# The last token group's finish in a hybrid decoder layer: inputs ahead, statistics by halves, and an adding transfer

## The chip, the cores and the metric

The kernel runs on one core of one Trainium2 chip. The metric is the device time of one execution in microseconds (us); lower is better. Times inside the profile are counted from the start of the span, which is the time from the first to the last instruction of the profiled execution.

## The reference

One layer of a hybrid decoder, in fp32, for 2048 prompt tokens and 64 sample tokens of width 2048:

```python
z = rms_norm(x, pre_g)
proj = z @ w_in
...
out = jnp.concatenate([br, bs], axis=-1) @ w_out
y = x + rms_norm(out, post_g)
```

Between the two products stand a causal convolution with a gated linear recurrence (branch `br`, 1024 wide) and a spatial gating in chunks of 128 tokens (branch `bs`, 1024 wide). What matters here is the last line: each row of `out` (one token) is divided by the root of the mean of its squares, multiplied by the vector `post_g` over the 2048 columns, and added to the row of `x`.

## The kernel before

The 2048 prompt tokens are worked in four groups of 512. Group 0 (with the sample tokens) has a path of its own; groups 1 to 3 go through one list of steps, `steps2`, 196 per group. A step is the matmuls with one weight block of 128x1024. Each fp32 operand is split into a high and a low part in the fp32r type (`hi_one`, ScalarE, line 184; `lo_one`, VectorE, line 192), and each product is three matmuls. The products use a scheme of seven half-size products in place of eight, named in `PROD` (B11, P4, B21, P2, P1, P3, B22) with the activation factors in `ACTS` (A11, A22, A12, E, D1, D3, F). The factors live in two pools, `zhi` (A11 and A22) and `zlo`, four slots for each factor, and are built once for the output product of a group.

The output product of a group is two wide products, `o0` and `o1` (`wide`), for columns 0 to 1023 and 1024 to 2047. Each has 7 times 4 steps of 2.8 us. After each of the seven products `take_product` and `evac` move what is finished from PSUM to SBUF by way of `put_o`. It makes tiles of 128 tokens by 512 columns: `c` is the block of 128 tokens (0 to 3), `half` is `c // 2`, and `qq` the quarter of the columns (0 to 3). Two blocks of one half share a tile of the pool `dbl` (13 buffers). `put_o` also has ScalarE square the tile and add up its rows into `oss` (line 963). The quarters of half 1 are all there after P3, those of half 0 only after B22, which gives half 0 of `qq` 3.

The order of all work is written by hand. A loop over steps `s` issues, in this order: weight loads up to step s + 5 (SyncE's queue), the high parts up to s + 2, then `early[s]` and `tasks[s]` (`at2` puts a call into `tasks`), the low parts up to s + 2, the step's matmuls, and `late[s]`. Each engine works off its own instructions in that order. `G`, `V`, `U`, `O` and `R2` are the step numbers at which a group, its v product, its u products, `o0` and `o1` begin; for the last group `R2` + 28 is the end of the list. SyncE issues the weight loads, and GpSimd (`side`) the other transfers of these groups.

For groups 1 and 2 the finish runs beside the next group: `out_rstd` makes the row factors (`ors`, with `rsqrt_small`, line 146 on), `load_gq` brings 1024 columns of `post_g` to all partitions (line 983), `finish_scale` multiplies (line 1000), `finish_add` has GpSimd issue a transfer that adds x from HBM onto the tile (line 1004), and `finish_store` stores it (line 1007).

For the last group nothing runs beside it. `load_gq` is called in the last steps, `out_rstd` two steps after the last product, and behind the loop `last_finish` is called 16 times (`qq` outer, `c` inner): SyncE loads a 128x512 tile of x (line 1012), VectorE multiplies the tile by the factor and the gain (line 1013) and adds x (line 1014), and SyncE stores the result (line 1015). The x tile is one of the pool `dbl`.

Of the kernel before, what the change touches and what calls it, by code (L numbers as in the profile page):

```python
# [9 lines left out]
F32 = mybir.dt.float32  # L10
F32R = mybir.dt.float32r
AF = mybir.ActivationFunctionType
ALU = mybir.AluOpType
AX = mybir.AxisListType

P = 128
D = 2048
# [9 lines left out]
NG = PROMPT // TP  # L27
# [4 lines left out]
Q = 512  # L32
# [19 lines left out]
def hybrid_layer(ctx: ExitStack, tc: tile.TileContext, a):  # L52
    nc = tc.nc
# [4 lines left out]
    mp = ctx.enter_context(tc.tile_pool(name="mp", bufs=2))  # L58
# [13 lines left out]
    def dbl(name, dt=F32):  # L72
        return dp.tile([P, 2, DW], dt, tag="dbl", name=name)
# [7 lines left out]
    def bank(name):  # L81
        return ps_g.tile([P, 512], F32, tag="gm", name=name)
# [10 lines left out]
    side = nc.gpsimd  # L93
# [42 lines left out]
    hcar = cp.tile([P, NH], F32, name="hcar")  # L136
    ccar = cp.tile([P, NH, 3], F32, name="ccar")
# [3 lines left out]
    state = {}  # L141

    def rsqrt_small(ss, n, out, name):
        w = ss.shape[-1]
        s = mp.tile([P, 2, 8], F32, tag="rsm", name=f"rsm{name}")
        m, q = s[:ss.shape[0], 0, :w], s[:ss.shape[0], 1, :w]
        nc.vector.tensor_scalar(m, ss, 1.0 / n, EPS, op0=ALU.mult, op1=ALU.add)
        nc.scalar.activation(q, m, AF.Sqrt)
        nc.vector.reciprocal(out, q)
        nc.vector.tensor_mul(q, out, out)  # L150
        nc.vector.tensor_mul(q, q, m)
        nc.vector.tensor_scalar(q, q, -0.5, 1.5, op0=ALU.mult, op1=ALU.add)
        nc.vector.tensor_mul(out, out, q)
# [544 lines left out]
    def mm_wide(key, r, u, bks):  # L698

        h, l = state["w", key]  # L700
        cont = PROD[r] in ("B21", "B22")
        for kl in range(2):
            kk = 2 * u + kl
            t = state["Z", ACTS[r], kk // 2]
            wh, wl = h[:, kl * Q:(kl + 1) * Q], l[:, kl * Q:(kl + 1) * Q]
            for b in range(2):
                zh, zl = (t[:, i, kk % 2, b * P:(b + 1) * P] for i in range(2))
                for n_pass, (zz, w) in enumerate(((zh, wh), (zh, wl), (zl, wh))):
                    nc.tensor.matmul(bks[b], zz, w, start=(not cont and kk == 0 and n_pass == 0),  # L709
                                     stop=(kk == HALF - 1 and n_pass == 2), skip_group_check=True)  # L710
# [4 lines left out]
    def evac(r, bk, tmp, put):  # L715

        k = PROD[r]
        if k == "B11":
            nc.scalar.activation(tmp["U"], bk["a"], AF.Copy)
        elif k == "B21":  # L720
            put(0, 0, bk["a"], None, None)
        elif k == "P2":
            nc.vector.tensor_sub(tmp["U"], bk["b"], tmp["U"])
        elif k == "P1":
            nc.scalar.activation(tmp["D"], bk["d"], AF.Copy)
        elif k == "P3":
            w = put(0, 1, tmp["U"], bk["c"], ALU.subtract, False)
            put(1, 1, w, tmp["D"], ALU.add)
            put(0, 1, bk["e"], w, ALU.subtract)
        elif k == "B22":  # L730
            put(1, 0, bk["d"], tmp["U"], ALU.add)

    steps2 = []
    early, tasks, late = defaultdict(list), defaultdict(list), defaultdict(list)

    def at2(s, f, *args):

        tasks[s].append((f, *args))
# [23 lines left out]
    def wide(g, name, kind, q, put):  # L762

        bks, tmp = {}, {}

        def mm(r, u, key):
            b = BANK[PROD[r]]
            if u == 0 and b not in bks:
                bks[b] = [bank(f"w{g}{name}{b}{i}") for i in range(2)]
            mm_wide(key, r, u, bks[b])  # L770

        def take_product(r, i):
            if i == 0 and r == 0:
                tmp["U"] = dbl(f"U{g}{name}")
            elif i == 0 and PROD[r] == "P1":
                tmp["D"] = dbl(f"D{g}{name}")
            evac(r, {x: y[i] for x, y in bks.items()}, {x: y[:, i, :TP] for x, y in tmp.items()},
                 lambda n, half, *args: put(n, half, i, tmp, *args))

        for r, k in enumerate(PROD):  # L780
            for u in range(4):
                steps2.append((mm, r, u, (g, kind, q, u, k)))
            for i in range(2):
                early[len(steps2) + (i if k != "P1" else 0)].append((take_product, r, i))

    def take(dst, ps, other, op, func=None):

        if op is None:
            nc.scalar.activation(dst, ps, func or AF.Copy)
            return  # L790
        nc.vector.tensor_tensor(dst, ps, other, op=op)
        if func is not None:
            nc.scalar.activation(dst, dst, func)
# [151 lines left out]
    def put_o(g, q):  # L945
        fresh = {}

        def put(n, half, i, tmp, ps, other, op, last=True):
            if ("oss", g) not in state:
                state["oss", g] = mp.tile([P, 4, 4], F32, tag="oss", name=f"oss{g}")  # L950
            if n == 0:
                if half not in fresh:
                    fresh[half] = dbl(f"o{g}_{q}_{half}")
                t = fresh[half]
            else:
                t = tmp["U" if half == 0 else "D"]
            c, qq = 2 * half + i, 2 * q + n
            o = t[:, i, :Q]
            take(o, ps, other, op)
            if not last:  # L960
                return o
            s = mp.tile([P, Q], F32, tag="junk", name=f"oq{g}_{c}_{qq}", bufs=1)
            nc.scalar.activation(s, o, AF.Square, accum_out=state["oss", g][:, c, qq:qq + 1])
            if g == NG - 1:
                state["o", g, c, qq] = o
            elif q == 1:
                state["fin", g, half, qq] = t
            elif i == 1:
                sp = hp.tile([P, 2, Q], F32, name=f"o{g}_{qq}_{half}")
                side.dma_start(sp, t[:, :, :Q])  # L970
                state["osp", g, half, qq] = sp
        return put
# [13 lines left out]
    def gq(qq):  # L986
        return state["gq", qq // 2][:, qq % 2, :Q]

    def rows(name, g, half, qq):
        return a[f"{name}{g}"][half * TH:(half + 1) * TH, qq * Q:(qq + 1) * Q].rearrange("(b p) c -> p b c", p=P)  # L990
# [15 lines left out]
    def finish_store(g, half, qq):  # L1006
        side.dma_start(rows("y", g, half, qq), state.pop(("fin", g, half, qq))[:, :, :Q])

    def last_finish(g, c, qq):
        o = state["o", g, c, qq]  # L1010
        x = dbl(f"lx{g}_{c}_{qq}")[:, 0, :Q]
        nc.sync.dma_start(x, a[f"xt{g}"][c * P:(c + 1) * P, qq * Q:(qq + 1) * Q])
        nc.vector.scalar_tensor_tensor(o, o, state["ors", g][:, c:c + 1], gq(qq), op0=ALU.mult, op1=ALU.mult)
        nc.vector.tensor_add(x, x, o)
        nc.sync.dma_start(a[f"y{g}"][c * P:(c + 1) * P, qq * Q:(qq + 1) * Q], x)

# [64 lines left out]
    for hp_ in range(0, NH, 2):  # L1083
        i = jobs.index(("gr", NH + hp_ + 1))
# [18 lines left out]
    for n, u in enumerate(units):  # L1103
        t = 60 + 20.5 * n
# [26 lines left out]
    for n, step in enumerate(steps):  # L1131
        for f, *args in by_step[n]:
            f(*args)
        job, i = step[0]
# [12 lines left out]
    zlo = ctx.enter_context(tc.tile_pool(name="zlo", bufs=4, reuse_waits="tile"))  # L1147
    zhi = ctx.enter_context(tc.tile_pool(name="zhi", bufs=4, reuse_waits="tile"))
# [12 lines left out]
    def combine(key, c, j, s):  # L1161

        at2(s, z_hi, key, c, j)
        at2(s + 1, z_lo, key, c, j)

    for g in range(1, NG):
        G = len(steps2)
        V, U, O, R2 = G + 56, G + 84, G + 140, G + 168
        for n, us in enumerate(XG):
            quad(g, f"xg{n}", us, put_xg(g, 2 * n))  # L1170
            e, k = len(steps2), (g, 2 * n)
# [15 lines left out]
            for t, (f, *args) in zip(ts, ((mul, ("i", *k), ("xc", *k)), (lru_exp, *k), (lru_sq, *k), (lru_mult, *k),  # L1187
                                          (act, ("t", *k), AF.Sqrt), (mul, ("i", *k), ("t", *k)),
                                          (lru_scan, *k, 0), (lru_scan, *k, 1), (lru_end, *k))):
                at2(e + t, f, *args)  # L1190
        wide(g, "v", "w_v", 0, put_v(g))
        if g == 1:
            for j in range(KT):
                t = 4 + 3 * j // 2 if j < 10 else V + 11 + 2 * (j - 10)
                at2(t, finish0_load, j)
                t = max(t + 3, 9)
# [3 lines left out]
        else:  # L1200
            at2(G - 1, load_gq, g - 1, 1)
            for n in range(4):
                k = (g - 1, (1, 1, 0, 0)[n], (3, 2, 2, 3)[n])
# [4 lines left out]
            for n in range(4):  # L1208
                k = (g - 1, n % 2, n // 2)
# [7 lines left out]
        for n, us in enumerate(UG):  # L1217
            quad(g, f"ug{n}", us, put_ug(g, 2 * n))
            e, k = len(steps2), (g, 2 * n)
# [20 lines left out]
            combine(key, "F", j, O + 18 + j)  # L1240
        for q in range(2):
            wide(g, f"o{q}", "w_or", q, put_o(g, q))
        at2(len(steps2) + 2, out_rstd, g)
        if g + 1 < NG:
            for n in range(8):
                at2(O + 2 + 3 * n // 2, stat_load, g + 1, n)
# [9 lines left out]
            for j in range(4):  # L1256
# [8 lines left out]
                combine(key, "D3", j, R2 + 23 + j)  # L1265
                at2(R2 + 21 + j, pre, key, "F", j)
                combine(key, "F", j, R2 + 26 + j)
    for q in range(2):
        at2(len(steps2) - 3 + 2 * q, load_gq, NG - 1, q)
    late[4].append((norm_a, "o"))  # L1270
    late[7].append((norm_b, "o"))

# [1 line left out]
    with tc.manual_schedule():  # L1274
        for s in range(len(steps2) + 4):
# [7 lines left out]
                f(*args)  # L1283
            for f, *args in late[s]:
                f(*args)
    g = NG - 1
    for qq in (0, 1, 2, 3):
        for c in range(4):
            last_finish(g, c, qq)
    nc.gpsimd.dma_start(a["o_cp"], ccar)  # L1290
    nc.gpsimd.dma_start(a["o_hp"], hcar)


def _layout(inp):
# [70 lines left out]
```

## Time and profile before

| | |
|---|---|
| Median of 3 runs | 2644.31 us (2639.09 to 2648.97) |
| The profiled execution | 2642.0 us, its span 2640.0 us |
| TensorE, its weight loads | busy 2523.5 us, 2321.1 us |
| VectorE, ScalarE, GpSimd | busy 1767.9 us, 1390.9 us, 339.9 us |
| Transfers | 587.12 MB, mean 222 GB/s over the span |
| Queue of SyncE, queue of GpSimd | 44.3% and 22.4% of the 16 transfer engines' span |

How to read it: the span is cut into stretches by what TensorE does. Group 0 takes the first third, groups 1 to 3 about 590 us each. Only in the last stretch, behind the last matmul, does TensorE have nothing to do, and there the other engines and the transfers set the time. PE is TensorE, DVE is VectorE, ACT is ScalarE, POOL is GpSimd, SP is SyncE; an engine with a q behind it is its queue of instructions that only issue or wait.

### The profile page before, as it was taken

What the parts mean: (1) busy time and instruction counts of PE and PEld (TensorE: products, weight loads), DVE (VectorE), ACT (ScalarE), POOL (GpSimd) and SP (SyncE); (2) the same over time, 40 slices, a digit from 0 to 9 for tenths busy, and PEclk for the clock granted to TensorE, in tenths of its full rate; (3) what the DMA queues carried; (4) which work ended last, traced back from release to release, by engine and by line L of the source; (5) the groups of instructions that cost most, each with busy time, mean ns of one, the idle gap of its engine ahead of it and who ended that gap; (6) DMA issues with size and microseconds to landing.
All of it is one profiled execution on the core that took longest, in us unless ns stands there. A gap on an engine that the chain in (4) does not pass through costs nothing.

```text
span 2640.0 us, 41631 instructions
## 1 busy us (share of the span) xinstructions
PE 2523.5 (96%) x16710; PEld 2321.1 (88%) x16710; DVE 1767.9 (67%) x2293; ACT 1390.9 (53%) x1778; POOL 339.9 (13%) x492
## 2 busy tenths in 40 slices
PE   7999999899998999999999999999999899999994
PEld 6999789899988998899878898899878898899883
DVE  7885255545457687656888586656788686666855
ACT  5445331123234577645766577645765577555642
POOL 4332023323331200100100200000100200000000
PEclk9999999999998999999999999999999999999997
DMA  6994378865864855756876955556776965555555
GB/s 224 342 342 174 118 262 307 313 247 196 315 235 151 280 183 178 239 180 182 266 260 210 299 192 163 184 180 189 269 238 216 297 191 165 184 183 177 185 190 191
DMA packets 168802, 587.12 MB, mean 222 GB/s; under 512 B 19344, under 2 KB 19904, under 8 KB 168608
## 3 DMA queue, kind: packets, MB, share of 16 engines
q1 hardware_dynamic: 110064, 383.36, 44.3%
q0 software_dynamic: 58544, 201.11, 22.4%
q8 instruction: 130, 2.13, 0.3%
q14 instruction: 64, 0.52, 0.1%
HBM read 494.92 MB, written 89.47 MB: 221 GB/s over the span
## 4 chain that ended last, share of the span: by engine, by line
PE 72%; DMA 10%; DVE 7%; ACT 6%; issue 4%; POOL 1%; SPq 0%; DVEq 0%; ACTq 0%; POOLq 0%
PE gm0out L363 6%; PE gm0v L374 4%; PE gm0gr L363 4%; PE gm0gs L363 3%; PE gm0xr L363 2%; DMA wraw_c_P<-P_c 1%; DMA pB22c<-w_in 1%; PE gm0u L363 1%; PE g L849 1%; PE sp L552 1%; PE w3vd L709 1%; DVE wl_c_B L192 1%; PE w2o1a L709 1%; PE w1o1a L709 1%; PE w2o0a L709 1%
## 5 line engine op out<-in xcount | busy, mean ns | idle before, releaser
L184 ACT ACTIVATE wh_c_P<-wraw_c_P 128x1024 fp32r<-128x1024 f32 x192 | 203.2, 1059 | 277.0 <-DMA wraw_c_P<-P_c 69.3
L192 DVE TENSOR_TENSOR wl_c_P<-wraw_c_P,wh_c_P 128x1024 fp32r<-128x1024 f32 x192 | 234.7, 1223 | 113.4 <-ACT wh_c_P L184 111.5
L192 DVE TENSOR_TENSOR wl_c_B<-wraw_c_B,wh_c_B 128x1024 fp32r<-128x1024 f32 x144 | 175.5, 1222 | 86.9 <-ACT wh_c_B L184 86.8
L184 ACT ACTIVATE wh_c_B<-wraw_c_B 128x1024 fp32r<-128x1024 f32 x144 | 151.9, 1056 | 140.2 <-DMA wraw_c_B<-w_in 44.1
L192 DVE TENSOR_TENSOR wl_w_or_P<-wraw_w_or_P,wh_w_or_P 128x1024 fp32r<-128x1024 f32 x96 | 117.5, 1223 | 50.1 <-ACT wh_w_or_P L184 49.7
L184 ACT ACTIVATE wh_w_or_P<-wraw_w_or_P 128x1024 fp32r<-128x1024 f32 x96 | 101.5, 1057 | 84.6 <-DMA wraw_w_or_P<-P_w_or 20.8
L184 ACT ACTIVATE wh_w_or_B<-wraw_w_or_B 128x1024 fp32r<-128x1024 f32 x72 | 76.1, 1058 | 79.6 <-DMA wraw_w_or_B<-w_or 18.4
L363 PE MATMUL gm0out<-c0l,wh_out 128*128 128x288 f32 x512 | 111.9, 300 | 1.2 <-DVE c0l L158 1.1
L363 PE MATMUL gm0out<-c0h,wh_out 128*128 128x288 f32 x512 | 110.4, 297 | 0.9 <-ACT wh_out L184 0.9
L192 DVE TENSOR_TENSOR wl_w_or_B<-wraw_w_or_B,wh_w_or_B 128x1024 fp32r<-128x1024 f32 x72 | 88.0, 1222 | 34.6 <-ACT wh_w_or_B L184 34.3
L363 PE MATMUL gm0out<-c0h,wl_out 128*128 128x288 f32 x512 | 110.2, 297 | 0.5 <-DVE wl_out L192 0.5
L363 PEld LDWEIGHTS gm0out<-c0l,wh_out 128*128 128x128 f32 x512 | 83.1, 190 | 2.6 <-DVE c0l L158 1.9
L363 PEld LDWEIGHTS gm0out<-c0h,wl_out 128*128 128x128 f32 x512 | 83.1, 190 | 1.2 <-DVE wl_out L192 0.7
L363 PEld LDWEIGHTS gm0out<-c0h,wh_out 128*128 128x128 f32 x512 | 83.0, 189 | 1.2 <-ACT wh_out L184 1.1
L613 POOL DMA_DIRECT2D xs<-xt x24 | 12.8, 536 | 510.5 <-ACT wh_c_P L184 259.1
L192 DVE TENSOR_TENSOR wl_w_v_P<-wraw_w_v_P,wh_w_v_P 128x1024 fp32r<-128x1024 f32 x48 | 58.5, 1222 | 28.2 <-ACT wh_w_v_P L184 28.2
L184 ACT ACTIVATE wh_out<-wraw_out 128x1024 fp32r<-128x1024 f32 x32 | 33.7, 1056 | 81.6 <-PE gm0out L363 53.9
L184 ACT ACTIVATE wh_w_v_P<-wraw_w_v_P 128x1024 fp32r<-128x1024 f32 x48 | 49.9, 1054 | 46.8 <-DMA wraw_w_v_P<-P_w_v 30.1
L192 DVE TENSOR_TENSOR wl_out<-wraw_out,wh_out 128x1024 fp32r<-128x1024 f32 x32 | 41.1, 1286 | 42.9 <-ACT wh_out L184 42.8
L363 PE MATMUL gm0xr<-z0h,wh_xr 128*128 128x288 f32 x256 | 56.5, 302 | 8.1 <-ACT wh_xr L184 5.4
L374 PE MATMUL gm0v<-wl_v,z0h 128*128 128x512 f32 (+1 forms) x160 | 63.5, 397 | 0.0
L374 PE MATMUL gm0v<-wh_v,z0l 128*128 128x512 f32 (+1 forms) x160 | 63.4, 396 | 0.0
(1598 smaller groups left out, 8553.6 us busy)
## 6 DMA issues: line engine op xcount, KB each, us to landing
wraw_c_P<-P_c SPq DMA_DIRECT2D x192, 512.0 KB, 3.9
wraw_c_B<-w_in SPq DMA_DIRECT2D x144, 512.0 KB, 4.2
wraw_w_or_P<-P_w_or SPq DMA_DIRECT2D x96, 512.0 KB, 4.2
wraw_w_or_B<-w_or SPq DMA_DIRECT2D x72, 512.0 KB, 4.0
wraw_w_v_P<-P_w_v SPq DMA_DIRECT2D x48, 512.0 KB, 3.6
wraw_w_v_B<-w_v SPq DMA_DIRECT2D x36, 512.0 KB, 3.3
wraw_out<-w_out SPq DMA_DIRECT2D x32, 512.0 KB, 4.8
xs<-xt POOLq DMA_DIRECT2D x24, 512.0 KB, 6.5
```

Source lines behind the costliest of these rows:

```text
L184: nc.scalar.activation(h[:, sl], raw[:, sl], AF.Copy)
L192: nc.vector.tensor_sub(l[:, sl], raw[:, sl], h[:, sl].bitcast(F32))
L363: nc.tensor.matmul(p[:, :n], w, zz[:, o:o + n], start=(k == 0 and n_pass == 0), stop=(k == KT - 1 and n_pass == 2))
L374: nc.tensor.matmul(p[:n], zz[:, c * P:c * P + n], w, start=(k == 0 and n_pass == 0), stop=(k == KT - 1 and n_pass == 2))
L552: nc.tensor.matmul(p[:, c * P:(c + 1) * P], state["vn", c, h // 4][:, vs], wst[:, h, :], start=True, stop=True)
L613: side.dma_start(x, a[f"xt{g}"][c * P:(c + 1) * P, b * W:(b + 1) * W])
L709: nc.tensor.matmul(bks[b], zz, w, start=(not cont and kk == 0 and n_pass == 0), stop=(kk == HALF - 1 and n_pass == 2), skip_group_check=True)
L849: nc.tensor.matmul(p, ww[:, ws], xx[:, i, :TP], start=n_pass == 0, stop=n_pass == 2)
```

## The change

The finish of the last group is taken apart and put into the list of steps.

- `last_x` has GpSimd load x, eight tiles of 256 tokens by 512 columns (512 KB), into slots of the factors A11 (half 1) and A22 (half 0) after these were read for the last time. `load_gq` moves from the last steps to steps R2 + 1 and R2 + 10.
- `last_gain` multiplies a tile by `post_g` without the row factor, in place, for all but one tile ahead of the last product's end. The tile of half 0, `qq` 3, is written to another tile.
- `last_rstd` makes the row factors for one half at a time: half 1 in step R2 + 26, half 0 in R2 + 28.
- Half 1 (`last_scale`): ScalarE multiplies by the row factor, GpSimd issues a transfer that adds the tile onto the x tile (both on chip), and SyncE stores it, 512 KB at a time.
- Half 0 (`last_both`): VectorE multiplies by the row factor and adds x in one instruction, and ScalarE issues the store, 256 KB at a time.
- The two halves of the last product's put are taken in one step. The stores of the two small state outputs `o_cp` and `o_hp` move into the list at V + 20.

```diff
@@
-                early[len(steps2) + (i if k != "P1" else 0)].append((take_product, r, i))
+                at_once = k == "P1" or (k == "B22" and g == NG - 1 and name == "o1")
+                early[len(steps2) + (0 if at_once else i)].append((take_product, r, i))
@@
-            if g == NG - 1:
-                state["o", g, c, qq] = o
-            elif q == 1:
+            if q == 1 or g == NG - 1:
                 state["fin", g, half, qq] = t
@@
-    def last_finish(g, c, qq):
-        o = state["o", g, c, qq]
-        x = dbl(f"lx{g}_{c}_{qq}")[:, 0, :Q]
-        nc.sync.dma_start(x, a[f"xt{g}"][c * P:(c + 1) * P, qq * Q:(qq + 1) * Q])
-        nc.vector.scalar_tensor_tensor(o, o, state["ors", g][:, c:c + 1], gq(qq), op0=ALU.mult, op1=ALU.mult)
-        nc.vector.tensor_add(x, x, o)
-        nc.sync.dma_start(a[f"y{g}"][c * P:(c + 1) * P, qq * Q:(qq + 1) * Q], x)
+    def last_x(half, qq):
+        x = state["lx", half, qq] = zhi.tile([P, 2, Q], F32, tag=("zA22", "zA11")[half], name=f"lx{half}_{qq}")
+        side.dma_start(x, rows("xt", NG - 1, half, qq))
+
+    def last_gain(half, qq, away=False):
+        o = state["fin", NG - 1, half, qq][:, :, :Q]
+        t = zlo.tile([P, 2, Q], F32, tag="zE", name=f"og{half}_{qq}") if away else o
+        nc.vector.tensor_mul(t, o, gq(qq).unsqueeze(1).to_broadcast([P, 2, Q]))
+        state["og", half, qq] = t
+
+    def last_rstd(half):
+        sv = mp.tile([P, 2], F32, tag="osv2", name=f"osvl{half}")
+        r = state["lors", half] = mp.tile([P, 2], F32, tag="ors2", name=f"orsl{half}")
+        nc.vector.reduce_sum(sv, state["oss", NG - 1][:, 2 * half:2 * half + 2, :], axis=AX.X)
+        rsqrt_small(sv, D, r, f"ol{half}")
+
+    def last_scale(half, qq):
+        o, x = state["og", half, qq], state["lx", half, qq]
+        for i in range(2):
+            nc.scalar.activation(o[:, i], o[:, i], AF.Copy, scale=state["lors", half][:, i:i + 1])
+        side.dma_start(x, o, accum_op=ALU.add)
+        nc.sync.dma_start(rows("y", NG - 1, half, qq), x)
+
+    def last_both(half, qq):
+        o, x = state["og", half, qq], state["lx", half, qq]
+        y = rows("y", NG - 1, half, qq)
+        for i in range(2):
+            nc.vector.scalar_tensor_tensor(x[:, i], o[:, i], state["lors", half][:, i:i + 1], x[:, i],
+                                           op0=ALU.mult, op1=ALU.add)
+            nc.scalar.dma_start(y[:, i], x[:, i])
@@
-        at2(len(steps2) + 2, out_rstd, g)
+        if g < NG - 1:
+            at2(len(steps2) + 2, out_rstd, g)
@@
-    for q in range(2):
-        at2(len(steps2) - 3 + 2 * q, load_gq, NG - 1, q)
+    at2(V + 20, nc.gpsimd.dma_start, a["o_cp"], ccar)
+    at2(V + 20, nc.gpsimd.dma_start, a["o_hp"], hcar)
+    at2(R2 + 1, load_gq, NG - 1, 0)
+    at2(R2 + 10, load_gq, NG - 1, 1)
+    for n in range(4):
+        at2(R2 + 5 + n, last_x, 1, n)
+        at2(R2 + 9 + n, last_x, 0, n)
+        at2(R2 + 5 + n, last_gain, n % 2, n // 2)
+    at2(R2 + 15, last_gain, 0, 2)
+    at2(R2 + 26, last_rstd, 1)
+    for qq in (2, 3):
+        at2(R2 + 26, last_gain, 1, qq)
+    for qq in range(4):
+        at2(R2 + (27 if qq < 2 else 29), last_scale, 1, qq)
+    at2(R2 + 28, last_gain, 0, 3, True)
+    at2(R2 + 28, last_rstd, 0)
+    for qq in range(4):
+        at2(R2 + 29, last_both, 0, qq)
@@
-    g = NG - 1
-    for qq in (0, 1, 2, 3):
-        for c in range(4):
-            last_finish(g, c, qq)
-    nc.gpsimd.dma_start(a["o_cp"], ccar)
-    nc.gpsimd.dma_start(a["o_hp"], hcar)
```

## Rows read from the trace of the kernel before

**Rows 1.** The page, busy time of TensorE and its share of the span.

```profile
PE 2523.5 (96%) x16710; PEld 2321.1 (88%) x16710; DVE 1767.9 (67%) x2293; ACT 1390.9 (53%) x1778; POOL 339.9 (13%) x492
```

**Rows 2.** The chain that ended last, 2440 to 2640: start, us, what.

```profile
2591.14 10.51 PE w3o1d L709 x45
...
2603.95 1.28 ACT L148
...
2606.49 0.04 DVE o L1013
```

**Rows 3.** Stretch 2620 to 2640: length, busy by engine, TensorE clock, transfer share, GB/s.

```profile
2620.00:2640.00 20.00, 0.00 (x0) 0.00 (x0) 9.32 (x14) 0.00 (x0) 0.00 (x0) 0.50 0.71 242
```

**Rows 4.** Waits, 2602 to 2640: total us, times, longest.

```profile
DVE lx L1014 <- DMA lx<-xt: 7.9, 7, 3.2
```

**Rows 5.** What touches the x tiles: ns min/median/max, first and last start.

```profile
L1012 SPq DMA_DIRECT2D lx<-xt x16: 327/410/467, 2589.4 to 2630.9; - x16
L1015 SPq DMA_DIRECT2D y<-lx x16: 332/343/478, 2608.5 to 2636.3; - x16
```

**Rows 6.** Timeline of SyncE's queue, 2490 to 2640: start, us, what.

```profile
2579.52 8.73 SPq L176 DMA_DIRECT2D wraw_w_or_B<-w_or  x4
...
2589.40 1.38 SPq L1012 DMA_DIRECT2D lx<-xt  x3
```

**Rows 7.** Stretches of groups 1 to 3, columns as in rows 3.

```profile
2075.60:2089.00 13.40, 13.13 (x104) 12.83 (x104) 7.78 (x10) 7.69 (x9) 2.95 (x4) 1.00 1.07 318
...
1903.00:1911.00 8.00, 8.00 (x35) 6.17 (x34) 5.76 (x8) 3.33 (x6) 3.62 (x5) 1.00 0.98 359
1910.00:1940.00 30.00, 28.01 (x117) 21.27 (x116) 26.54 (x40) 17.60 (x26) 2.83 (x4) 1.00 0.77 272
2050.00:2095.00 45.00, 39.24 (x298) 37.80 (x297) 29.27 (x40) 21.51 (x25) 12.10 (x14) 0.96 1.06 345
```

**Rows 8.** Timeline, 2585 to 2640, ScalarE and VectorE.

```profile
2585.57 1.06 ACT L184 ACTIVATE wh_w_or_B<-wraw_w_or_B 128x1024 fp32r<-128x1024 f32 x1 [1.74 <-PE w3o1c L709]
...
2586.67 1.23 DVE L192 TENSOR_TENSOR wl_w_or_B<-wraw_w_or_B,wh_w_or_B 128x1024 fp32r<-128x1024 f32 x1 [1.57 <-ACT wh_w_or_B L184]
...
2596.59 0.19 ACT L963 ACTIVATION_READ_ACCUMULATOR oq<-o 128x1 f32 x1
...
2601.68 1.39 DVE L791 TENSOR_TENSOR U3o<-w3o1d,U3o 128x512 f32<-128x512 f32 x2 [4.61 <-PE w3o1d L709]
...
2606.49 1.42 DVE L1013 SCALAR_TENSOR_TENSOR o<-o,ors,gq 128x512 f32<-128x512 f32 x2
```

**Rows 9.** The post_g loads (512 KB), from issue to landing.

```profile
DMA to landing us min/median/max: 5.7/6.2/10.9
```

**Rows 10.** Groups by line, shapes apart: busy us, mean ns, idle before.

```profile
L861 ACT ACTIVATE t<-r,rate_p 128x512 f32<-128x512 f32 x24 | 15.9, 712 | 0.0
...
L1013 DVE SCALAR_TENSOR_TENSOR o<-o,ors,gq 128x512 f32<-128x512 f32 x8 | 5.8, 748 | 0.0
```

**Rows 11.** Timeline of GpSimd in groups 2 and 3: adding transfers and stores.

```profile
1440.12 1.24 POOL L1004 DMA_DIRECT2D D1o<-xt  x1 [84.64 <-DVE D1o L1000]
...
2084.10 0.72 POOL L1007 DMA_DIRECT2D y<-fo  x1 [3.34 <-DMA fo<-xt]
...
2089.02 0.72 POOL L1007 DMA_DIRECT2D y<-fo  x1 [3.47 <-DMA fo<-xt]
```

**Rows 12.** Transfers, 2612 to 2640: GB/s in 40 slices; queue, packets, MB, share.

```profile
GB/s 328 205 152 158 190 114 178 287 375 354 401 342 351 272 287 208 263 167 252 266 395 342 255 363 354 287 278 366 275 293 173 88 225 196 202 184 348 26 0 0
...
q1 hardware_dynamic: 3767, 6.84, 73.2%
```

**Rows 13.** Transfers, 2034 to 2038: GpSimd's queue, packets, MB, share.

```profile
q0 software_dynamic: 265, 0.57, 77.5%
```

**Rows 14.** Transfers, 1440.1 to 1443.2: the only queue that moved anything.

```profile
q1 hardware_dynamic: 193, 0.72, 89.4%
```

**Rows 15.** The adding transfers of line 1004 (512 KB), from issue to landing.

```profile
DMA to landing us min/median/max: 9.2/13.8/15.7
```

## The prediction

> **What bounds the kernel now.** The page's first part comes first: TensorE is busy for 96% of the span [rows 1], so what the kernel does elsewhere counts only where TensorE stands still. The chain that ended last, in order of time, shows the one long place [rows 2]: the last product of the last group runs until 2601.65 us, and from there to the end of the span at 2640.0 us no TensorE work is left. That tail is 38.3 us. Its first 4.8 us are the row statistics, to 2606.49; the other 33.5 us are the finish, a chain of loads of x, adds and stores. The stretch table says what the finish is made of: from 2620 to 2640 VectorE is busy 9.3 of 20 us and the transfer engines 0.71 [rows 3]. The waits of the tail name the reason: VectorE waits 7.9 us for x [rows 4]. Only three loads of x are issued ahead (at 2589.40); the other 13 share SyncE's queue with the stores, up to the last store at 2636.3 [rows 5, 6]. So the finish moves 13 loads and 16 stores of 256 KB one behind the other, with gaps.
>
> **The change, part by part.**
>
> *x and post_g ahead.* Eight loads of 512 KB go to GpSimd's queue, each into a slot of the A11 or A22 factors, which comes free when the last reading product's step ends. The seven products of the last half are 11.2 us each, four steps of 2.8; the first begins at 2523.9, six products before 2591.14 [rows 2]. So one load goes out per step, from about 2526.7; GpSimd has nothing else to do then, and behind a load that waits there are only the next loads. The first gain load follows on SyncE's queue. In these eight steps (22.4 us) the transfers are 8 weights, 8 x and one gain, 17 x 0.524 = 8.9 MB. A stretch of the group before, with as many loads beside the weights, moved 359 GB/s [rows 7], so 8.9 MB need 24.8 us, 2.4 us more than there are. Weights have room for that: a weight is asked for at 2579.52, first read at 2585.57, split until 2587.9 and used at 2591.14 [rows 2, 6, 8], so it may take 6.1 us to land and 3.2 us more before TensorE waits. In the group before, a stretch with this load lost 2.0 of 30 us of TensorE [rows 7], with VectorE at 26.5 of 30 us; here it has one split (1.23 us) and one gain product (about the same, the same shape) per 2.8 us. I take 0 and keep 0 to 2.0 us.
>
> The gain load costs SyncE 0.4 us ahead of a weight load. It goes out behind the weight load of its step, at about 2529.5, and lands 5.7 to 10.9 us later [rows 9]; the first gain product stands on VectorE at about 2537.5 (18 steps before the split that ends at 2587.9), so it may wait up to 2.9 us. Queued behind it is a weight split: it would end near 2542.9, still ahead of its use at 2543.5 (seven steps after 2523.9). Cost 0. The gain products themselves hide under TensorE (one split and one product are 2.5 of 2.8 us); without that cover each is 1.2 us. The two small state outputs were issued by GpSimd when their data was ready, and are again; nothing stands behind them for a long time. Cost 0.
>
> *Statistics of half 1.* Its last squares are read out at 2596.78 [rows 8]. From the start of the table load to the finished factors took 2.5 us (2603.95 to 2606.49) [rows 2]; the table load waits for nothing, so the factors of half 1 are ready at 2596.8 + 2.5 = 2599.3. Then ScalarE scales two tiles, two passes of 0.71 each [rows 10], about 1.3 us with their overlap: the first adding transfer can be issued at 2600.7 and the second at 2602.0. ScalarE is free again when VectorE ends the last put (the first at about 2602.4) [rows 8], so the squares of half 0 are not late. VectorE does two gain products of 1.2 us from 2599.3 to 2601.8, 0.1 us past the time at which the last put began: 0.1 us.
>
> *Statistics and finish of half 0.* Puts to 2603.2, last gain product to 2604.4, squares to 2604.0, then the same small chain without a table load (1.6 us; a second load would add 1.28): factors at 2606.0. Eight fused steps of 0.75 us, 0.71 apart (two in 1.42) [rows 8, 10], end at 2611.7. That replaces 32 instructions on VectorE and their waits. The stores are issued by ScalarE. No row shows that; the nearest are 0.34 us on SyncE [rows 5] and 0.72 to 0.75 on GpSimd [rows 11]. I take 0.35, the hardware queue's price; at 0.75 it would still keep pace with the fused steps. Four scaling passes stand ahead of the stores (to 2607.5), and behind a store that waits only the next ones. The second put of the last product is taken in the same step as the first; nothing lay between them before: 0.
>
> *The transfers of the tail.* These set the end. Plain transfers in the tail before: 6.84 MB took 73.2% of 28 us, so 0.334 MB/us, and 0.785 us for 256 KB, 1.57 for 512 KB [rows 12]. No row shows an adding transfer from on-chip memory to on-chip memory; the nearest are the adding transfers from HBM in the group before. In a stretch in which the GpSimd queue moved almost nothing else, 0.57 MB took 77.5% of 4 us, 0.184 MB/us, so 2.85 us for 512 KB [rows 13]. I take that, as the old value has still to be read; lower bound 1.57 us (a plain copy), upper bound 4.9 us (between two stores that each waited for an add to land, 2084.10 and 2089.02, with weights alongside) [rows 11]. The sum of the tail: 4 adds x 2.85 = 11.4, 4 stores x 1.57 = 6.3, 8 stores x 0.785 = 6.3, together 24.0 us of all engines; when full, the share reads 1.07 [rows 7], so 22.4 us. It starts late: after an issue at 1440.12, GpSimd's queue moved nothing until 1443.2 at the earliest [rows 11, 14]. I take 3.3 us: 2600.7 + 3.3 = 2604.0. From then on one queue or another always has work: the second add is behind the first, from 2608 the stores of half 0 come faster than they are moved, and the last two adds are issued at 2606.4 and 2607.7. So data end at 2604.0 + 22.4 = 2626.4. Before, data stopped some 1.4 to 2.1 us ahead of the end of the span [rows 12]; with 2.0 us, and 0.5 us because the last store of half 1 must wait for its add, the span ends at 2629: 11 us less.
>
> So the finish is no longer held by the order of one queue, but by bytes: 4 MB of stores as before and 2 MB of adds at half speed, in place of 3.4 MB of loads.
>
> **Numbers.** The profiled execution took 2642.0 us with a span of 2640.0; 11 less is 2631.0. The median of the runs shown is 2.3 us above it, so 2644.3 - 11 = 2633 us. What a measurement of this kernel can tell from no change is about 0.5%, 13.2 us, so the line is at 2631.1.
>
> **The rivals.**
>
> *Adds at the price of plain copies* (1.57 us): 6.3 + 12.6 = 18.9, over 1.07 is 17.6 us; the end comes at 2604.0 + 17.6 + 2.0 = 2623.6, so 2628. For it: the source is on chip. Against it: 0.184 against 0.334 MB/us. Chance 0.17.
>
> *The transfer engines do not bind*, and the end is a chain of waits: the last add, issued at 2607.7, lands after 9.2 us, the least of the group before [rows 15], and its store takes 3.7 us, as from the last issue at 2636.3 to the end [rows 5], and 0.8 more for twice the bytes: 2621.4, 18.6 us less, so 2626. Against it: 22.4 us of work do not fit between 2604.0 and 2619.4. Chance 0.05. The Trainium skill, "DMA: Bandwidth & Descriptors", section "Anatomy of one DMA — SWDGE (gpsimd) path", fits a transfer as about 2.0 us plus its bytes over 436 GB/s, whatever it does; by that the 6.3 MB would be an estimated 14.4 us, and this rival would hold. The trace does not agree: at 0.184 MB/us it moves adds at less than half that rate.
>
> *The loads ahead stall TensorE.* By 2.0 us, as in the group before, to 5.8, as in the stretch 2050 to 2095 with adds in flight (39.24 of 45 us busy) [rows 7]. The gain is then 5 to 9 us: 2635 to 2639. For it: weights, x and gain ask for more than 359 GB/s. Against it: 9.3 us of room. Chance 0.15.
>
> *Slower: adds one at a time.* If each add waited for the one before to land, at the 13.8 us from issue to landing of the group before [rows 15], four take 55 us from 2600.7 and the last store 4.5: 2660, 20 us more, so 2664. It decides against the change from about 8.7 us per add (2600.7 + 4 x 8.7 + 4.5 = 2640). Against it: adds landed 4.9 us apart with weights alongside [rows 11]. Chance 0.06.
>
> **Chances.** The forecast itself has 0.57; its own range is 2629 to 2637, and a third of it lies under 2631.1. Faster by over 0.5%: 0.17 + 0.05 + 0.19 = 0.41. Within 0.5%: 0.38 + 0.15 = 0.53. Slower: 0.06. The range takes in the first three rivals, with some 2 us above the last of them for the spread of runs (10 us between three runs), and leaves out the slower one: 2625 to 2641.
>
> **What would show it.** Right: no load of x asked for after 2552; TensorE's last product ending within 1 us of 2602.3; half 1's factors near 2599.3; fused steps of 0.75 us ending near 2612; the transfer share at 1.0 or above from 2604 to 2626 with less than 300 GB/s; adds at some 0.18 MB/us. Wrong: a share well under 1 in that stretch (the chain binds), adds at 0.33 MB/us, TensorE idle between 2530 and 2560, or GpSimd issuing its fourth add long after 2608.

## The result, and the profile after

The changed kernel takes 2620.82 us (median of 4 runs, 2616.0 to 2626.4), the kernel before beside it 2641.7 us (4 runs, 2638.42 to 2648.97): a ratio of 0.9921 [0.9903, 0.994]. That is 20.9 us less (15.9 to 25.6 by the interval), where 11 were forecast, and 4 us below the range. The profiled execution took 2626.4 us, its span is 2624.7 us (15.3 us less than the span before).

TensorE's share has not moved; the page's first part answers to [rows 1]:

```profile
PE 2515.9 (96%) x16710; PEld 2314.8 (88%) x16710; DVE 1761.6 (67%) x2284; ACT 1396.5 (53%) x1787; POOL 350.7 (13%) x504
```

The chain that ended last, in order of time (start us, us, what), answers to [rows 2]:

```profile
2543.46 11.39 PE w3o1a L709 x48
2554.84 11.20 PE w3o1b L709 x48
...
2588.44 10.51 PE w3o1d L709 x45
...
2603.17 0.75 DVE lx L1039
```

The last product ends at 2588.44 + 10.51 = 2598.95. The tail from there to the end of the span is 25.75 us; it was 38.35. So the tail gives 12.6 us. The rest of the 20.9 us must lie ahead of the last product's end, where the change was not meant to save anything.

The timeline of the other engines shows the order of the tail (start us, us, engine, line, operation, tiles, count; in brackets the idle time before it); it answers to [rows 8]:

```profile
2594.10 1.28 ACT L148 ACT_TABLE_LOAD   x1
...
2596.42 0.16 DVE L153 TENSOR_TENSOR orsl<-orsl,rsmol 128x2 f32<-128x2 f32 x1
...
2596.62 1.34 ACT L1030 ACTIVATE o<-o,orsl 128x512 f32<-128x512 f32 x2 [1.02 <-DVE orsl L153]
...
2598.39 1.23 POOL L1031 DMA_DIRECT2D lx<-o  x1 [53.80 <-ACT o L1030]
2598.98 1.40 DVE L792 TENSOR_TENSOR U3o<-w3o1d,U3o 128x512 f32<-128x512 f32 x2
...
2599.62 1.27 POOL L1031 DMA_DIRECT2D lx<-D3o  x1
...
2602.97 0.16 DVE L153 TENSOR_TENSOR orsl<-orsl,rsmol 128x2 f32<-128x2 f32 x1
2603.17 1.41 DVE L1039 SCALAR_TENSOR_TENSOR lx<-o,orsl,lx 128x512 f32<-128x512 f32 x2
...
2603.56 14.95 SPq L1032 DMA_DIRECT2D y<-lx  x4
2603.80 1.21 POOL L1031 DMA_DIRECT2D lx<-o  x1 [2.91 <-ACT o L1030]
2603.95 15.46 ACTq L1041 DMA_DIRECT2D y<-lx  x8
2605.02 1.22 POOL L1031 DMA_DIRECT2D lx<-D3o  x1
2607.15 1.41 DVE L1039 SCALAR_TENSOR_TENSOR lx<-og,orsl,lx 128x512 f32<-128x512 f32 x2
```

All computing has ended by 2608.6 (2607.15 + 1.41); what follows is transfers. The stretches of 2 us say how full they are (PE, PEld, DVE, ACT, POOL busy us, then TensorE's granted clock, the transfer engines' share, GB/s); they answer to [rows 3]:

```profile
2598.00:2600.00 2.00, 1.65 (x8) 0.98 (x6) 1.86 (x3) 1.42 (x3) 1.61 (x2) 1.00 0.00 0
2600.00:2602.00 2.00, 0.00 (x0) 0.00 (x0) 1.84 (x4) 1.27 (x5) 0.89 (x1) 1.00 1.00 173
...
2620.00:2622.00 2.00, 0.00 (x0) 0.00 (x0) 0.00 (x0) 0.00 (x0) 0.00 (x0) 0.50 1.05 361
2622.00:2624.00 2.00, 0.00 (x0) 0.00 (x0) 0.00 (x0) 0.00 (x0) 0.00 (x0) 0.50 0.29 112
```

In every stretch from 2600.0 to about 2622.6 the share is 1.0 or more: the transfer engines have no time to spare there. The view of the queues for 2600 to 2624.7 (24.7 us; packets, MB, share of 16 engines) splits them and answers to [rows 12]. q0 carries the adding transfers, q1 SyncE's stores, q10 ScalarE's:

```profile
q0 software_dynamic: 1088, 2.10, 49.0%
q1 hardware_dynamic: 1088, 2.10, 24.0%
q10 hardware_dynamic: 1152, 2.10, 23.9%
```

The four adds take 0.49 x 24.7 = 12.1 us of all engines, 3.0 us for 512 KB. The stores take 5.9 us per 2.10 MB, 1.48 for 512 KB, half as much.

### The profile page after: what moved, and what is told of

Its sections match the earlier page's. It is cut to its first block, busy times and chain, and to the rows that moved or that the text cites. A ratio compares the mean times of both kernels' runs of the same rounds, so it can differ in the third digit from the quotient of the medians.

```text
span 2624.7 us, 41603 instructions
## 1 busy us (share of the span) xinstructions
PE 2515.9 (96%) x16710; PEld 2314.8 (88%) x16710; DVE 1761.6 (67%) x2284; ACT 1396.5 (53%) x1787; POOL 350.7 (13%) x504
## 4 chain that ended last, share of the span: by engine, by line
PE 71%; DMA 10%; DVE 8%; ACT 5%; issue 4%; POOL 1%; SPq 0%; DVEq 0%; ACTq 0%; POOLq 0%
PE gm0out L363 7%; PE gm0v L374 4%; PE gm0gr L363 4%; PE gm0xr L363 2%; PE gm0gs L363 2%; DVE wl_c_B L192 1%; DMA wraw_c_P<-P_c 1%; PE gm0u L363 1%; DMA wraw_w_or_P<-P_w_or 1%; PE g L850 1%; DMA pB22w_v<-w_v 1%; DMA wraw_c_B<-w_in 1%; PE sp L552 1%; PE w3o1a L709 1%; PE w3vd L709 1%
```

## The experiments

From here on the tail is counted from the start of the last matmul to the end of the span of the profiled run: 38.06 us before, 25.45 after. Three sets of runs, each on one chip with its own runs of the kernel before (medians 2636.56, 2637.9 and 2639.06 us), ask three questions: what works outside the tail, which part of the change works in it, and whether less would do better.

### Outside the tail: the place of the buffers

Apart from two small stores at V + 20, only one thing in the diff reaches the work ahead of the group's last wide product, `o1`. `last_rstd` uses two new tags, `osv2` and `ors2`, in the pool of small tiles (`mp`). Four buffers of 32 bytes each for the two together make 128 bytes per partition, so every pool made later, with the factors in `zhi` and `zlo` among them, starts 128 bytes further on; the weight tiles stay. The theory is that the place of the buffers gives the time outside the tail. The rivals are the spread of runs, and something that the moved transfers do.

**The kernel before, unchanged**, for what two equal kernels can differ by.

> The kernel before, once more, for a second trace. Two theories for what the shorter time has beyond the tail. Theory P (place): the four new 32-byte buffers of the row factors move every buffer behind them by 128 bytes, and the products of 48 matmuls of 256 columns run in 5.60 us in place of 5.63 to 5.70. Theory D (drift): stalls and rates ahead of the last group's finish differ from one execution to the next, whatever the program. P expects products of 5.63 to 5.70 us in the u stage of group 3 again, and a ratio of 1.00. D expects that they may as well be 5.60. Both expect a tail (last product's end to span end) of 38 us.

Measured: 2635.75 us against 2636.56, 1.0002 [0.9992, 1.0013], with 12 and 17 runs; tail 37.6 us. With as many runs a tenth of a per cent can be told.

**The kernel before, moved by 128 bytes**, with two unused tiles and nothing else:

```diff
+    for tag in ("osv2", "ors2"):
+        nc.vector.memset(mp.tile([P, 2], F32, tag=tag, name=f"pad{tag}"), 0.0)
```

> The kernel before with four unused 32-byte buffers in the same pool, so that every buffer behind it stands where it stands in the changed kernel. P expects products of 5.60 us in the u stages, 6 to 8 us less time (ratio 0.997 to 0.998), and a tail of 38 us. D expects a ratio of 1.000 within 0.001 and the same tail.

Measured: 2627.47 us, 0.9964 [0.9952, 0.9976], 9.5 us less (6.3 to 12.7) with a tail of 38.77. Two idle tiles, written once, make the kernel faster. The mean granted clock is no reason: over the runs it is 0.982 for both kernels.

**The change, not moved**: the old tags in place of the new ones.

```diff
-        sv = mp.tile([P, 2], F32, tag="osv2", name=f"osvl{half}")
-        r = state["lors", half] = mp.tile([P, 2], F32, tag="ors2", name=f"orsl{half}")
+        sv = mp.tile([P, 2], F32, tag="osv", name=f"osvl{half}")
+        r = state["lors", half] = mp.tile([P, 2], F32, tag="ors", name=f"orsl{half}")
```

> The changed kernel with the row factors of the halves in the existing buffers, so that every buffer stands where it stands in the kernel before. P expects a tail of 25 to 26 us, products of 5.63 to 5.70 us, and 12 to 13 us less than before (ratio 0.995). D expects the same tail and the same ratio as the changed kernel itself.

Measured: 2622.8 us, 0.9952 [0.994, 0.9964], 12.7 us less (9.5 to 15.8); tail 25.13. That is the tail's gain and no more, so the moved transfers bring nothing outside the tail.

**The change again**, on the same chip.

> The changed kernel once more. P expects 18 to 21 us less than before (ratio 0.992 to 0.993) with products of 5.60 us in the u stages; D expects the tail's 12.6 us (ratio 0.995) as the mean, with some us of spread from one execution to the next.

Measured: 2613.52 us, 0.992 [0.9907, 0.9933], 21.1 us less; tail 25.14. The two parts, 12.7 and 9.5, add up to 22.2.

A part of what the 128 bytes do can be seen in the u stages, whose products are 48 matmuls with 256 columns. The stretch from 2320 to 2380 lies inside the last of them in both kernels (columns as above). First the kernel before, then the same moved by 128 bytes:

```profile
2320.00:2380.00 60.00, 60.00 (x510) 60.00 (x510) 35.34 (x39) 32.12 (x33) 0.00 (x0) 1.00 0.59 183
```

```profile
2320.00:2380.00 60.00, 60.00 (x518) 60.00 (x517) 35.21 (x38) 31.33 (x35) 0.00 (x0) 1.00 0.55 177
```

TensorE is busy all the time in both, at a granted clock of 1.00, and gets through 518 matmuls in place of 510. In the chains a product is 5.60 us in place of 5.70. The three fences are the kernel before (with an earlier product of 5.63), the kernel before moved, and the change not moved:

```profile
2303.80 5.63 PE q3ug0d L695 x48
...
2345.11 5.70 PE q3ug1d L695 x48
```

```profile
2338.82 5.60 PE q3ug1d L698 x48
```

```profile
2339.34 5.70 PE q3ug1d L695 x48
```

The change itself has 5.60. Added up over the three u stages (from the first matmul of each u product 0 to the first of `o0`): 501.2 and 501.4 us in the two profiles of before, 500.9 for the change not moved; 496.1 for before moved, 495.2 and 495.1 in the two of the change. So in the kernel before moved the u stages account for 5.3 us of the 9.5, whose interval begins at 6.3. No stage was found that holds the remainder: other stages differ by more than that from one profile to the next (group 1's second u product begins between 1132 and 1144 us, in moved and unmoved kernels alike).

Two more ask what has to move. **Half the shift** (64 bytes, one unused tag) and **the factors alone** (a pool of 128 bytes ahead of `zlo` and `zhi`, the pool of tiles `dbl` draws on left where it was):

```diff
+    for tag in ("osv2",):
+        nc.vector.memset(mp.tile([P, 2], F32, tag=tag, name=f"pad{tag}"), 0.0)
```

```diff
+    gap = ctx.enter_context(tc.tile_pool(name="gap", bufs=1))
+    nc.vector.memset(gap.tile([P, 32], F32, name="gap"), 0.0)
```

> The kernel before with two unused 32-byte buffers: a shift by 64 bytes in place of 128. If any other place than that of the kernel before helps, products of 5.60 us and a ratio of 0.996. If the distance matters, products between 5.60 and 5.70 us, and a ratio of its own; if it is the existence of more buffers and not their place, as with four: 0.996.

> The kernel before with a gap of 128 bytes ahead of the two pools of activation factors alone; every other buffer stands where it stood. If the place of the factors, which TensorE reads, sets the pace, products of 5.60 us and a ratio of 0.996. If it is the place of the working tiles that VectorE and ScalarE use beside it, products of 5.63 to 5.70 us and a ratio of 1.000.

Measured: 64 bytes give 2635.24 us, 0.9985 [0.9975, 0.9995], with u products of 5.68 us and u stages of 499.7; the factors alone give 2632.92 us, 0.9975 [0.9962, 0.9988], with products of 5.60 and 5.65 and u stages of 496.2. One product of each chain, half the shift first:

```profile
2335.98 5.68 PE q3ug1d L698 x48
```

```profile
2335.38 5.65 PE q3ug1d L695 x48
...
2376.67 5.60 PE q3ug2d L695 x48
```

So the place of the factors, relative to the buffers that stayed (the weights among them), carries the u stages' part, and 64 bytes do not do what 128 do. By what mechanism the place sets the pace was not found.

### In the tail: which part works

**x and post_g ahead, nothing else**, on the kernel before (the four `last_x` and gain lines of the change in the list; not moved):

```diff
     def last_finish(g, c, qq):
...
-        x = dbl(f"lx{g}_{c}_{qq}")[:, 0, :Q]
-        nc.sync.dma_start(x, a[f"xt{g}"][c * P:(c + 1) * P, qq * Q:(qq + 1) * Q])
+        x = state["lx", c // 2, qq][:, c % 2]
```

> The kernel before with one part of the change: x and post_g are loaded as in the changed kernel, and the finish stays as it was (statistics of all tokens behind the last product, two passes of VectorE per tile, stores on SyncE's queue). The theory is that the order of loads and stores in one queue held the finish of before. It expects VectorE without waits for x, 32 passes of 0.7 us behind the factors, a tail of 4.8 + 22 + 3.4 = 30 us, so 8 us less than before. The rival (the stores' bytes or the landing of each store bind anyway) expects a tail of 35 us or more. Both expect no loss of TensorE by the loads, or 2 us at most.

Measured: 2627.55 us, 0.9965 [0.9952, 0.9978]; tail 28.53, 9.5 us less. No load is left in the tail, so VectorE's 32 passes set the end; three lines of its chain, of a sequence that alternates without a wait for data:

```profile
2600.82 0.04 DVE o L1016
...
2618.61 1.32 DVE D3o L1016 x2
2619.93 0.60 DVE lx L1017
```

The transfer engines are half empty there (2600 to 2624):

```profile
q1 hardware_dynamic: 2304, 4.20, 49.6%
```

Three quarters of the tail's 12.6 us are had by this alone. The halves, the fused steps, ScalarE's scaling and the adds give the other 3.4 us (28.53 to 25.13).

**The adds as plain copies**; for half 1 the addition of x is left out:

```diff
-        side.dma_start(x, o, accum_op=ALU.add)
+        side.dma_start(x, o)
```

> The changed kernel with plain copies in place of the four adding transfers (the addition of x is left out for half 1). The theory is that the transfer engines set the end of the tail, and that an add costs them twice a copy. It expects GpSimd's queue at 1.5 us per 512 KB in place of 3.0, and a tail of 20 us in place of 25.7. The rival, that the chain of landings binds, expects a tail of 24 us or more.

Measured: 2605.8 us, 0.9882 [0.9865, 0.9899]; tail 19.39, 6 us less than with the adds. The queues from 2590 to 2608.6 (18.6 us):

```profile
q10 hardware_dynamic: 1152, 2.10, 31.2%
q1 hardware_dynamic: 1088, 2.10, 30.2%
q0 software_dynamic: 537, 1.94, 28.4%
```

q0 now takes 0.284 x 18.6 = 5.3 us for 1.94 MB, so 1.43 us for 512 KB in place of 3.0. The bytes are the same; it is the adding that costs double. The copies also go in half as many packets (537 for 1.94 MB, where the adds have 1088 for 2.10). That is unlikely to be the reason, as SyncE's stores after the change have 1088 packets too and take 1.48 us per 512 KB; an add in fewer packets was not run. Four times 1.57 us is 6.3, over a share of 1.06 it is 5.9: the tail's difference.

**No adds**: half 1 goes the way of half 0, its stores on SyncE.

```diff
-        at2(R2 + (27 if qq < 2 else 29), last_scale, 1, qq)
+        at2(R2 + (27 if qq < 2 else 29), last_both, 1, qq)
```

> The changed kernel with half 1 finished as half 0 is: VectorE's fused steps in place of ScalarE's scaling and the adding transfers, in the same steps of the list, with stores of 256 KB on SyncE's queue. The theory (the transfer engines bind, and the adds are half of their work) expects the transfers to need only 12 us of the tail; then VectorE binds, with 16 fused steps, and the tail is 19 us in place of 25.7. The rival (VectorE was relieved for a reason: its additional 5.7 us stand ahead of the last stores) expects 25 us or more.

Measured: 2614.13 us, 0.9913 [0.9894, 0.9932]; tail 19.67. VectorE does eight more fused steps, and the chain shows how little that is:

```profile
2594.53 2.65 DVE lx L1039 x4
2597.18 1.21 DVE U3o L792 x2
...
2602.46 6.62 DVE lx L1039 x10
```

It ends at 2609.1, and the span 5.5 us later, with the last stores. The adds took work off an engine that ended 16 us before the span did (2608.6 of 2624.7), and gave it to the transfer engines, which set the end.

**No adds and no halves**: the row factors of all tokens after the last product, against the kernel without adds (`last_rstd_all` calls `out_rstd` and hands its factors to both halves; not moved).

```diff
-    at2(R2 + 26, last_rstd, 1)
...
-    for qq in range(4):
-        at2(R2 + (27 if qq < 2 else 29), last_both, 1, qq)
...
-    at2(R2 + 28, last_rstd, 0)
+    at2(R2 + 28, last_rstd_all)
     for qq in range(4):
-        at2(R2 + 29, last_both, 0, qq)
+        for half in (1, 0):
+            at2(R2 + 29, last_both, half, qq)
```

> As the run without adds, but with the statistics of all tokens taken once, behind the last product. It leaves of the change the loads ahead, the gain ahead and the fused step. If the halves are worth what they let run early, the tail is longer than without adds by VectorE's four fused steps ahead of the last put and a table load, less the second chain of small steps: 20 us against 19. If the halves carry the change, it is 23 us or more.

Measured: 2618.23 us, 0.9931 [0.9913, 0.995]; tail 19.26, not longer than with halves. The chain:

```profile
2598.35 0.71 ACT L148
...
2600.89 3.40 DVE lx L1044 x5
2604.29 0.66 DVEq L1393
2604.95 6.63 DVE lx L1044 x10
```

Once the adds are gone, the halves are worth nothing that the tail shows. The 0.71 us of ScalarE (line 148) are a part of the table load for the square root.

### Less, and better

**One add only** (tile 1, 0), the others by `last_both`; the table for the square root loaded at R2 + 2; VectorE's waits for ScalarE filled with gain products and fused steps (moved as the change is):

```diff
+    at2(R2 + 2, sqrt_table)
...
+    at2(R2 + 27, last_scale, 1, 0)
+    at2(R2 + 27, last_both, 1, 1)
...
-            nc.scalar.dma_start(y[:, i], x[:, i])
+            (nc.sync if half else nc.scalar).dma_start(y[:, i], x[:, i])
```

> The changed kernel with one adding transfer left (half 1, first quarter); VectorE finishes the other tiles of half 1. The square root's table is loaded in step R2 + 2, and VectorE's gain products and fused steps fill its waits for ScalarE. If bytes and VectorE's passes share the tail as the runs so far say, 14 fused steps behind the last product and 15.5 us of transfers give a tail of 16.5 to 17.5 us, and a ratio of 0.988 to 0.989. If one add still holds up the stores, the tail is 19 us or more.

Measured: 2613.3 us, 0.99 [0.9879, 0.9922]; tail 20.95: a miss. SyncE's queue shows why, in the timeline:

```profile
2589.89 1.41 DVE L1053 SCALAR_TENSOR_TENSOR lx<-D3o,orsl,lx 128x512 f32<-128x512 f32 x2
...
2595.71 0.39 SPq L1046 DMA_DIRECT2D y<-lx  x1
...
2596.19 4.61 SPq L1055 DMA_DIRECT2D y<-lx  x6
```

Tile 1, 1 is finished at 2591.3, but its stores stand in the queue behind the store of tile 1, 0, which waits until 2595.71 for its add to land. The transfer engines are partly idle meanwhile (columns as above):

```profile
2594.00:2596.00 2.00, 0.00 (x0) 0.00 (x0) 1.90 (x7) 0.20 (x1) 0.00 (x0) 0.66 0.64 109
2596.00:2598.00 2.00, 0.00 (x0) 0.00 (x0) 1.97 (x5) 0.00 (x0) 0.00 (x0) 0.50 0.68 262
```

About a third of these 4 us is lost, 1.4 us, of a miss of 3.5 to 4.5 us in all. The queues from 2590 to 2612.4 (22.4 us) show most of the rest:

```profile
q10 hardware_dynamic: 1152, 2.10, 32.8%
q1 hardware_dynamic: 1136, 2.10, 31.3%
```

The stores take 7.3 + 7.0 = 14.4 us of all engines, where the same bytes took 5.9 + 5.9 after the change. That is 2.5 us more, at a share of about 1.08 some 2.3. In the run without adds they take 14.2 us as well, in the run without adds and halves 11.9. Why they cost more in these two is not shown. The next run leaves out the last add too.

**No adds, no halves, moved, the table early**: the kernel without adds and halves, with the two unused tags and

```diff
+    def sqrt_table():
+        nc.scalar.activation(warm, warm, AF.Sqrt)
...
+    at2(R2 + 2, sqrt_table)
```

> The run with whole statistics and no adds, with the buffers where the changed kernel has them and the square root's table loaded in step R2 + 2. The place theory expects products of 5.60 us in the u stages and 6 to 9 us less than the run without the shift, the table 1.0 us less: a tail of 18.2 us and a ratio of 0.989 to 0.990. The rival, that the shift acts through something of the changed finish, expects 5.63 to 5.70 us and a ratio of 0.993.

Measured: 2612.33 us, 0.989 [0.9869, 0.9911]; tail 18.60. The u products take 5.60 us, as the place theory expects of the moved kernel. The stretches show the stores binding from 2590 on, while VectorE still works (columns as above):

```profile
2588.00:2590.00 2.00, 0.00 (x0) 0.00 (x0) 2.00 (x4) 0.00 (x0) 0.00 (x0) 0.50 0.51 190
2590.00:2592.00 2.00, 0.00 (x0) 0.00 (x0) 2.00 (x5) 0.00 (x0) 0.00 (x0) 0.50 1.08 341
...
2598.00:2600.00 2.00, 0.00 (x0) 0.00 (x0) 0.04 (x1) 0.00 (x0) 0.00 (x0) 0.50 1.03 396
```

It has fewer parts than the change and its tail is 6.5 us shorter. Its ratio of 0.989 stands against 0.992 of the change, measured on another chip; the two intervals overlap a little, so the 6.5 us are shown in the tail and not in the medians.

## Why the prediction was wrong

**Loads ahead at no cost: right.** In the stretch of the loads TensorE loses nothing, at 337 GB/s where [rows 7] had 359:

```profile
2524.00:2552.00 28.00, 28.00 (x121) 22.28 (x119) 15.68 (x14) 11.52 (x14) 5.80 (x8) 1.00 0.93 337
```

One product of the seven is 0.2 us longer (11.39, the chain above). The first gain product waited 0.4 us where up to 2.9 were allowed. The rival of a stalled TensorE falls.

**The factors: right.** Those of half 1 were forecast 2.35 us ahead of the last product's end (2599.3 against 2601.65) and came 2.37 ahead (2596.58 against 2598.95). Those of half 0 were to come 4.35 us behind it and came 4.2 behind. The last fused step was to end 10.05 us behind it and ended 9.6 behind, at 0.75 us a step.

**The transfers: the sum right, one term off.** The sum of 24.0 us was 23.9 (12.1 + 5.9 + 5.9); adds at 3.0 us per 512 KB against 2.85 from [rows 13], the share 1.06 against 1.07 [rows 7]. So two rivals fall: adds at the price of plain copies, and transfer engines that do not bind. The Trainium skill, "DMA: Bandwidth & Descriptors", section "Anatomy of one DMA — SWDGE (gpsimd) path", whose fit for one transfer gave the second rival an estimated 14.4 us, does not agree with the 22.6 us of full engines here. The Trainium skill, "DMA: Bandwidth & Descriptors", section "Rules for kernel authors", says that an accumulating transfer reads its destination and writes it later; the copy in the add's place, 1.43 us against 3.0, agrees with that. Adds one at a time fall as well: the second was issued 1.2 us behind the first (2599.62), ahead of the first one's data, and the engines were full from the start.

The term that failed is the start, "I take 3.3 us" from issue to first data. The add issued at 2598.39 had its first packets between 2600.0 and 2600.4, so 1.6 to 2.0 us. The 3.3 came from an issue into an idle queue of GpSimd, but at a time when SyncE's queue took 89.4% of the engines [rows 14]; ahead of 2600.0 they moved nothing (the stretch 2598 to 2600 above). That this made the difference is not shown. That makes the tail 1.1 us shorter; another 0.4 us lies behind the last data (2.1 us in place of 2.5). Together they are nearly the difference between the 27.35 us forecast and 25.75.

**The step that failed** is the last one: "The profiled execution took 2642.0 us with a span of 2640.0; 11 less is 2631.0". It takes for granted that everything ahead of the finish keeps its time. The diff allocates two tags, and that moves buffers from which the matmuls read. With the tail's 12.6 us alone the sum gives 2631.7 us, inside the range; the 9.5 us of the moved kernel before put it at 2622, near the 2620.8 measured. (The sum also starts from 2644.3, and the runs beside the result put the kernel before at 2641.7.) No term, no rival and no part of the range stood for the move of the buffers, so its share of the chance of faster (0.41) was missing too.

The trace of before held a sign of it: products of 48 matmuls with 512 columns took 11.2 us (the prediction has the number), half of which is 5.60 for 256 columns, and the u products took 5.63 and 5.70 with TensorE never idle. So they ran slower than the wide products did per column. Why, and which way a shift would move it, could not have been told from that.

## What to carry to other kernels

A new tag in an early pool moves all later buffers; on this kernel, bound by TensorE, that alone was worth three quarters of what the change itself brought (0.36% and 0.48%), so compare matmul durations of stages that an edit doesn't touch, and time the old kernel with the same shift. In a tail that ends in stores, count the transfer engines' time before handing them arithmetic: an add by transfer costs twice a copy, and its store holds up the finished ones queued behind it. Bring the inputs in ahead first; here that was three quarters of the tail's gain, and finishing every tile with one fused pass on VectorE gave a shorter tail (18.6 to 19.7 us) than the change's mix of engines and adds (25.1 to 25.5).

## What was not expected of the hardware

- The pace of 48 matmuls of 256 columns at a granted clock of 1.00 depends on where the operands stand in on-chip memory: 5.70 us, 5.68 with a shift of 64 bytes, 5.60 with 128 (one u product each of group 3).
- Issuing an adding transfer holds GpSimd for 1.21 to 1.27 us (the timeline after), a plain one of the same size for 0.72 us (in the run with copies).
- The same 4.2 MB of stores took 11.4 to 11.9 us of all transfer engines in the change, with plain copies and in the two runs without halves, and 14.2 and 14.4 us without adds and with one add. The cause is open.
- Of the moved kernel's 9.5 us, 5.3 lie in the u stages; the rest was not located. Kernels with the same shift and the same tail still differed in their medians by 8 us (2605.8 with plain copies, 2614.13 without adds), so a part of the time ahead of the tail stays unexplained, and conclusions on the tail rest on its own length. Part of such a spread goes with the granted clock: the change's two profiled executions, 2626.4 and 2612.31 us, have the same tail and the same u stages, and mean clocks of 0.981 and 0.985.
- The shift is there in every run all the same. The median less the tail is 2597.7 to 2599.0 us in the four runs without it (before again, the change not moved, loads ahead, no adds and no halves) and 2586.4 to 2594.5 in the six with 128 bytes, over three chips; for the pair of the result, measured apart from these, it is 2603.6 before and 2595.4 after.
